# First token pair loaded by halves and projected without its norm, head norms ahead of rotations, last tile in halves

## The chip, the cores and the metric

The kernel runs on one core of a Trainium2 chip. The metric is the device time of one execution in microseconds (us), the median of several runs. The engines are TensorE (PE in the profile, with its weight loads as PEld), VectorE (DVE), ScalarE (ACT), GpSimd (POOL) and SyncE (SP), which here only issues transfers. They run side by side, each in the order of its own instructions, and wait for each other by semaphores.

## What is computed

One encoder block over 2048 tokens of width 1024 and 16 learned tokens ahead of them, in float32. Only the start and the end matter here:

```python
hn = rms_norm(h, g_mix[i])
proj = hn @ w_in[i]                      # 1024 -> 512 q, 256 k, 256 v, 512 u
q = axial_rope(rms_norm(q, g_q[i]), ...)     # norm over each head's 128
k = axial_rope(rms_norm(k, g_k[i]), ...)
attn = block_attention(q, k, v)
four = fourier_mix(u, w_fourier[i])
h = h + concat(rms_norm(attn), rms_norm(four)) @ w_out[i]
h = h + square(relu(rms_norm(h) @ w_up[i])) @ w_down[i]
return rms_norm(h, g_final)[:, N_META:]
```

`rms_norm(x, g)` is `x * rsqrt(mean(x*x) + 1e-6) * g`.

## The kernel before

**Products.** Every float32 product is made of three faster ones (`mm3`, lines 79 to 81): each operand is split into a high part (a rounded copy, `hi`) and a low part (the rest, `lo`), and high by high, high by low and low by high are added in PSUM. A split is one copy on ACT and one subtraction on DVE (`Split`, lines 69, 70; with a column of gains as a scale, 72, 73).

**Stage 1.** Tokens are taken in eight pairs `j` of two tiles `a` of 128 rows. `load_x` issues a pair's two transfers of 512 KB. `prep(j)` norms the pair (`norm_x`, for the first one `norm_first`), turns it with 16 transposes on PE (`pt`, line 290) and splits the result into `hth`, `htl`. `proj_qkv(j)` makes q, k and v from it (`pq`, `pkv`), `proj_u(j)` the Fourier input u (`pu`, copied to `UA`). `post(j, a)` is a generator that squares the heads out of PSUM, takes their norms and rotates them with DVE, transposes them on PE (`ptq`, `ptk`) and stores them. The loop at line 589 runs the generators a step at a time between the projections by `side()`, so that the work of pair `j` lies beside the projections and the preparation of pair `j+1`.

The weights `w_in` come in pieces of 256 KB (`wraw`, line 225), eight for q, k and v of rows 0 to 511 first, then eight more and eight for u; each piece is split by one ACT and one DVE instruction into `wh`, `wl`. For the first pair `proj_qkv` runs over the rows of `w_in` outermost, with all four accumulators open, so PE can begin as soon as the first pieces are split. `wake()` (line 209) gives PE six products of a constant tile ahead of everything else.

**Order.** The code is written once; a scheduler orders each engine's instructions by it and by the waits. `tc.issue_after(i)` asks that an instruction stand behind `i` on its engine. SP issues its transfers in order; at most eight are under way, and the ninth waits for the first. All raw pieces and transposed splits live in one ring of 17 buffers (`t2k`), and token tiles in one of three (`x`). PSUM has four banks `mm` for products and four `tr` for transposes in this stage.

**The end.** The down projection of the MLP is worked off in groups; the last products (name "4" of group 3) finish token tiles 4 to 7 of the second half: per tile `t` twelve products of 512 columns, `add`, and `follow`: `square` on ACT, `norm` (a small DVE instruction, then a power on POOL), and `store` of the tile before it, which scales half the row on DVE and half on ACT and issues both to SP.

## Time and profile before

| | |
|---|---|
| median of 3 runs | 2295.94 us (2295.4 to 2296.68) |
| the profiled execution's own time | 2296.3 us |
| its span, first to last instruction | 2294.5 us |
| PE busy | 2280.1 us, 99% of the span |
| DVE, ACT, POOL busy | 75%, 56%, 8% |
| granted TensorE clock over the span | 0.999 |

The profile is of one execution. Its span is 1.8 us shorter than that execution's own time, and that time is 0.36 us above the median. Busy PE is an upper bound of work, since its instructions overlap: the record of a product of 512 columns is 0.39 us long, but in the chain of waits each takes 0.23 us.

### The profile page before, as it was taken

To read this page: it belongs to the slowest core of one execution; us is meant where nothing else is said; L and a number is where in the kernel's file an instruction comes from. 1 tells how busy PE (TensorE), PEld (TensorE's weight loads), DVE (VectorE), ACT (ScalarE), POOL (GpSimd) and SP (SyncE) were. 2 spreads that over 40 slices of the span, in tenths; PEclk is the share of its full clock that TensorE was granted. 3 is DMA by queue.
4 is the path that set the end of the run, shared out by engine and by line. 5 is a ranking of instruction groups with operands and counts; after the bars stand their busy time and mean duration, and the time that the engine had idled before them with its cause. 6 is when DMAs were issued, how large, how long until landed. Compare 5 with 4: busy or idle time off the path is not lost.

```text
span 2294.5 us, 29976 instructions
## 1 busy us (share of the span) xinstructions
PE 2280.1 (99%) x10834; PEld 1882.9 (82%) x10834; DVE 1716.6 (75%) x2444; ACT 1281.7 (56%) x2303; POOL 186.9 (8%) x235
## 2 busy tenths in 40 slices
PE   9999999999999999999999999999999999999998
PEld 7888988787888888888888888888888888888887
DVE  6435579999976877976887977885884656697786
ACT  6443355566665655665765775664665555543344
POOL 2212120222000000000000100000000000200000
PEclk9999999999999999999999999999999999999999
DMA  6343252543533222333242453324454444864442
GB/s 213 100 119 103 77 169 79 164 152 119 177 117 107 93 87 79 115 113 111 93 160 79 161 172 106 97 78 167 144 171 166 151 152 156 302 197 161 129 138 83
DMA packets 178069, 307.23 MB, mean 134 GB/s; under 512 B 14960, under 2 KB 63728, under 8 KB 177536
## 3 DMA queue, kind: packets, MB, share of 16 engines
q1 hardware_dynamic: 159280, 263.16, 35.2%
q0 software_dynamic: 18640, 42.16, 6.2%
q8 instruction: 85, 1.39, 0.3%
q14 instruction: 64, 0.52, 0.1%
HBM read 225.27 MB, written 79.99 MB: 133 GB/s over the span
## 4 chain that ended last, share of the span: by engine, by line
PE 95%; DVE 2%; ACT 1%; issue 1%; DMA 1%; POOL 0%; POOLq 0%; DVEq 0%; ACTq 0%
PE pdn L79 5%; PE pdn L81 5%; PE pdn L80 5%; PE pup L79 5%; PE pup L81 5%; PE pup L80 5%; PE s L79 3%; PE ux L79 3%; PE ux L80 3%; PE ux L81 3%; PE dx L81 2%; PE dx L79 2%; PE dx L80 2%; PE s L81 2%; PE s L80 2%; PE o L79 2%
## 5 line engine op out<-in xcount | busy, mean ns | idle before, releaser
L79 PE MATMUL pdn<-wh_dn,ah 128*128 128x512 f32 x512 | 201.7, 394 | 0.5 <-ACT r L1137 0.5
L79 PE MATMUL pup<-mTh,wh_up 128*128 128x512 f32 x512 | 201.7, 394 | 0.0
L80 PE MATMUL pup<-mTl,wh_up 128*128 128x512 f32 x512 | 200.8, 392 | 0.0
L81 PE MATMUL pup<-mTh,wl_up 128*128 128x512 f32 x512 | 200.5, 392 | 0.0
L80 PE MATMUL pdn<-wl_dn,ah 128*128 128x512 f32 x512 | 200.0, 391 | 0.0
L81 PE MATMUL pdn<-wh_dn,al 128*128 128x512 f32 x512 | 198.9, 392 | 0.0
L764 ACT COPY S<-s 128x512 f32<-128x512 f32 x256 | 148.7, 583 | 53.7 <-PE s L81 40.6
L69 ACT CAST wh_up<-wr_up 128x512 fp32r<-128x512 f32 x128 | 79.4, 620 | 164.3 <-PE pup L80 76.5
L823 DVE TENSOR_TENSOR S<-S,mb 128x1024 f32<-128x1024 f32 x128 | 155.9, 1229 | 8.7 <-ACT mb L794 8.5
L70 DVE TENSOR_TENSOR pl<-S,ph 128x512 fp32r<-128x512 f32 x196 | 132.8, 698 | 11.3 <-ACT ph L69 11.0
L69 ACT CAST wh_dn<-wr_dn 128x512 fp32r<-128x512 f32 x128 | 79.0, 620 | 107.3 <-PE pdn L81 52.5
L70 DVE TENSOR_TENSOR wl_up<-wr_up,wh_up 128x512 fp32r<-128x512 f32 x128 | 87.6, 687 | 67.7 <-ACT wh_up L69 62.9
L830 DVE TENSOR_TENSOR acc<-acc,S 128x1024 f32<-128x1024 f32 x110 | 134.6, 1223 | 2.6 <-ACT S L824 2.5
L824 ACT ACTIVATE S<-S 128x1024 f32<-128x1024 f32 x114 | 120.6, 1059 | 26.2 <-DVE S L823 25.7
L70 DVE TENSOR_TENSOR wl_dn<-wr_dn,wh_dn 128x512 fp32r<-128x512 f32 x128 | 87.3, 688 | 60.4 <-ACT wh_dn L69 52.0
L69 ACT CAST ah<-a 128x1024 fp32r<-128x1024 f32 x56 | 58.5, 1048 | 121.3 <-issue 62.7
L770 DVE TENSOR_TENSOR M<-M,S 128x1024 f32<-128x1024 f32 x96 | 117.5, 1224 | 9.1 <-ACT S L764 8.7
L69 ACT CAST ph<-S 128x512 fp32r<-128x512 f32 x196 | 118.2, 620 | 8.1 <-PE o L81 5.2
L79 PEld LDWEIGHTS pdn<-wh_dn,ah 128*128 128x128 f32 x512 | 96.2, 188 | 24.0 <-ACT r L1137 3.7
L79 PE MATMUL s<-q,kt 128*128 128x512 f32 (+1 forms) x272 | 114.2, 420 | 1.4 <-DMA q<-q_d 1.4
L81 PEld LDWEIGHTS pdn<-wh_dn,al 128*128 128x128 f32 x512 | 96.2, 188 | 19.7
L79 PEld LDWEIGHTS pup<-mTh,wh_up 128*128 128x128 f32 x512 | 96.2, 188 | 19.3 <-DVE h L1163 0.2
(339 smaller groups left out, 6413.4 us busy)
## 6 DMA issues: line engine op xcount, KB each, us to landing
wr_up<-in_w_up_dram SPq DMA_DIRECT2D x128, 256.0 KB, 2.8
wr_dn<-in_w_down_dram SPq DMA_DIRECT2D x128, 256.0 KB, 2.6
a<-s_d SPq DMA_DIRECT2D x42, 512.0 KB, 3.7
R<-in_w_up_dram SPq DMA_DIRECT2D x16, 1024.0 KB, 5.4
s_d<-s SPq DMA_DIRECT2D x64, 256.0 KB, 2.1
d<-in_w_down_dram SPq DMA_DIRECT2D x26, 512.0 KB, 5.0
s_d<-c SPq DMA_DIRECT2D x48, 256.0 KB, 2.3
x<-in_x_dram SPq DMA_DIRECT2D x16, 512.0 KB, 4.9
```

Source lines behind the costliest of these rows:

```text
L69: self.high = nc.scalar.copy(hi, src)
L70: self.low = nc.vector.tensor_tensor(lo, src, f32v(hi), op=ALU.subtract)
L79: nc.tensor.matmul(out, a[0], b[0], start=first, stop=False, skip_group_check=chain)
L80: nc.tensor.matmul(out, a[0], b[1], start=False, stop=False, skip_group_check=chain)
L81: nc.tensor.matmul(out, a[1], b[0], start=False, stop=last, skip_group_check=chain)
L764: nc.scalar.copy(S[:, i % 2], ps)
L770: nc.vector.tensor_tensor(M, M, S, op=ALU.max)
L823: nc.vector.tensor_tensor(S, S, mb, op=ALU.subtract)
L824: nc.scalar.activation(p, S, AF.Exp, scale=ISQ)
L830: nc.vector.tensor_tensor(acc, acc, p, op=ALU.add)
```

## The change

Loading and projecting the first pair: its two tiles are loaded in halves of 512 columns, the first two halves ahead of the first weights and the other two behind the weights of the first 128 rows. The tiles are not normed: transposes work on the raw tiles as they land. The norm's factor `rs` is computed later (`norm_first`, now called after the weights of q, k and v were split, its squares behind the last split of the transposed tiles) and enters where the results are read: in the heads' norms (whose own mean then needs `rs` squared, `rsq_0`), in v's copy, and, spread over partitions by two transposes on PE (`spread_first`), in the copy of u, which goes from ACT to DVE for this pair. The wake products fall from six to two. ACT gets a one-element activation at the start.

`post`: squares, head norms, their products and v's copy come first, then a step of the generator ends; the table of the rotation is loaded and multiplied on POOL only then, and the rotations follow. The squares' by-product goes into `qn` rather than `t1`. For the first pair `side()` runs `prep` of the next pair ahead of the pending `post` steps.

The end: the last tile's twelve products become two runs of twelve with 256 columns, the second into a PSUM bank of its own. The first half is squared on ACT, the second on DVE. Tile 6 is stored between. The last of the stores is issued by ACT rather than SP.

```diff
-WAKE = 6
+WAKE = 2
...
+    def load_first(h):
+
+        for a in range(2):
+            if h == 0:
+                xs[0, a] = tp.tile([P, D], F32, name=f"x_0_{a}", tag="x", bufs=3)
+            c = slice(h * 512, (h + 1) * 512)
+            nc.sync.dma_start(xs[0, a][:, c], x[a * P:(a + 1) * P, c])
+
+    load_first(0)
...
         sm = tp.tile([P, 2], F32, name="sm_0", tag="sm", bufs=2)
         nc.vector.tensor_tensor(sm, ss[:, :, 0], ss[:, :, 1], op=ALU.add)
-        rs = rstd_of(tp, sm, 2, D, "x")
-        for h in range(2):
-            for a in range(2):
-                v = xs[0, a][:, h * 512:(h + 1) * 512]
-                if a == 0:
-                    early[f"x0{h}"] = ins_of(nc.scalar.activation(v, v, AF.Copy, scale=rs[:, a:a + 1]))
-                else:
-                    early[f"x1{h}"] = ins_of(nc.vector.tensor_scalar(v, v, rs[:, a:a + 1], None, op0=ALU.mult))
+        rs = rstd_of(mid, sm, 2, D, "a")
+        sq = mid.tile([P, 2], F32, name="rsq_0", tag="hsm", bufs=4)
+        nc.vector.tensor_tensor(sq, rs, rs, op=ALU.mult)
+        nc.vector.tensor_scalar(sq, sq, 1.0 / HD, None, op0=ALU.mult)
+        raw0["rs"], raw0["sq"] = rs, sq
+
+    def spread_first():
+        ps = tbank("prs_0", (P, 256))
+        for a in range(2):
+            nc.tensor.transpose(ps[:, a * P:(a + 1) * P], bc(raw0["rs"][:, a:a + 1], [P, P]), ident)
+        raw0["b"] = t2k("rsb_0", [P, 1, 256], F32)
+        nc.scalar.copy(raw0["b"][:, 0], ps)
...
-                if j < 4:
+                if j == 0:
+                    nc.vector.tensor_tensor(UA[:, g, n0:n0 + 256], ps, bc(raw0["b"], [P, 2, 256]), op=ALU.mult)
+                elif j < 4:
                     nc.scalar.copy(UA[:, g, n0:n0 + 256], ps)
...
-        rs = rstd_of(tp, ss[:rows, h0:], 6 - h0, HD, f"h{h0}", rows)
+        rs = rstd_of(tp, ss[:rows, h0:], 6 - h0, HD if j else raw0["sq"][:, a:a + 1], f"h{h0}", rows)
+        if j == 0:
+            nc.vector.tensor_scalar(rs, rs, raw0["rs"][:, a:a + 1], None, op0=ALU.mult)
...
+        if j == 0:
+            nc.scalar.activation(vr, v, AF.Copy, scale=raw0["rs"][:, a:a + 1])
+        else:
+            nc.scalar.copy(vr[:rows], v)
+        yield
+        cs = tp.tile([P, 2, P], F32, name=f"cs_{t}", tag="cs", bufs=1)
+        nc.sync.dma_start(cs[:rows], c_rope[t * P:t * P + rows, :, :])
...
     for k in range(4):
         load_w(k, 0)
         load_w(k, 512)
+        if k == 0:
+            load_first(1)
...
+            if j == 0:
+                next(nxt, None)
             for g in list(pend):
                 if next(g, "end") == "end":
                     pend.remove(g)
-            next(nxt, None)
+            if j:
+                next(nxt, None)
...
-            nc.sync.dma_start(out[(8 + t) * P:(9 + t) * P, halves[h]], w)
+            eng = nc.scalar if t == 7 and w is z else nc.sync
+            eng.dma_start(out[(8 + t) * P:(9 + t) * P, halves[h]], w)
...
+            def ends(t):
+
+                products(t, slice(0, 256))
+                rest = ybank(f"dy4_{g}_{t}")
+                products(t, slice(256, 512), rest)
+                with tc.issue_after(ends_ahead[0]):
+                    add(t)
+                h = hs[o0 + t][:, halves[half]]
+                v = h[:, 256:]
+                sq = [small.tile([P, 2], F32, name=f"ese_{i}", tag="hss", bufs=8)[:, :1] for i in range(2)]
+                nc.scalar.activation(junks[0][:, :256], h[:, :256], AF.Square, accum_out=sq[0])
+                norm_part(o0 + t, sq[0])
+                store(*done.pop())
+                nc.vector.tensor_tensor(v, v, rest[:, 256:], op=ALU.add)
+                nc.vector.scalar_tensor_tensor(junks[1][:, 256:], v, 1.0, v, op0=ALU.mult, op1=ALU.mult, accum_out=sq[1])
+                norm(o0 + t, half, sq[1])
```

SP at the start of the program, before (x are token tiles, wraw the raw pieces of `w_in`, ident the unit matrix of the transposes; a wait on a DMAHW semaphore is for an earlier transfer):

```order
L169 DMA x_0_0_90<-in_x_dram 128x1024
L169 DMA x_0_1_92<-in_x_dram 128x1024
L174 DMA cols_94<-g_cols 128x24
L176 DMA ident_96<-c_id 128x128
L225 DMA wraw0_0_141<-in_w_in_dram 128x512
L225 DMA wraw512_0_143<-in_w_in_dram 128x512
```

and now:

```order
L178 DMA x_0_0_90<-in_x_dram 128x512
L178 DMA x_0_1_92<-in_x_dram 128x512
L182 DMA cols_94<-g_cols 128x24
L184 DMA ident_96<-c_id 128x128
L236 DMA wraw0_0_139<-in_w_in_dram 128x512
L236 DMA wraw512_0_141<-in_w_in_dram 128x512
L178 DMA x_0_0_90<-in_x_dram 128x512
L178 DMA x_0_1_92<-in_x_dram 128x512
```

The first two weight pieces now stand between the halves of the token tiles, and the last half is eighth where the sixth transfer stood, with the same bytes up to its end.

PE at the middle of the first pair's transposes, now (pt are their results; before, the same 16 stand together, with waits for ACT and DVE, which scaled the tiles):

```order
L306 MATMUL pt_0_1_166<-ident_96,x_0_1_92 128x128
L306 MATMUL pt_0_2_175<-ident_96,x_0_0_90 128x128 [waits DMAHW6_49]
L306 MATMUL pt_0_3_184<-ident_96,x_0_0_90 128x128
L306 MATMUL pt_0_2_175<-ident_96,x_0_1_92 128x128 [waits DMAHW7_49]
L306 MATMUL pt_0_2_175<-ident_96,x_0_0_90 128x128
L306 MATMUL pt_0_2_175<-ident_96,x_0_1_92 128x128
L306 MATMUL pt_0_3_184<-ident_96,x_0_1_92 128x128
L306 MATMUL pt_0_3_184<-ident_96,x_0_0_90 128x128
L306 MATMUL pt_0_3_184<-ident_96,x_0_1_92 128x128
L79 MATMUL pq_0_0_334<-wh1024_0_193,hth_0_0_162 128x512 [waits Activation_49]
```

The waits are now for the transfers themselves: two transposes stand behind the third half, six behind the fourth, and all products behind these.

ACT at the norm of the third pair (jk are squares of a token tile, the x lines its scaling, qt the split of transposed q, t1 or qn the heads' squares), before:

```order
L404 ACTIVATE t1_2_822,sq_2_820<-pq_1_0_675 128x128 [waits DVE_49,PE_49]
L404 ACTIVATE t1_2_822,sq_2_820<-pq_1_0_675 128x128
L69 CAST qt_0_705<-ptq_0_700 128x512 [waits PE_49]
L244 ACTIVATE jk_2_0_0_719,ss_2_0_718<-x_2_0_664 128x512 [waits DMAHW2_49,DVE_49]
L244 ACTIVATE jk_2_0_1_721,ss_2_0_718<-x_2_0_664 128x512 [waits DVE_49]
L244 ACTIVATE jk_2_1_0_731,ss_2_1_730<-x_2_1_666 128x512 [waits DMAHW2_49,Activation_49]
L249 ACTIVATE x_2_0_664<-x_2_0_664,rs_x_727 128x1024 [waits Activation_49,Pool_49]
L244 ACTIVATE jk_2_1_1_733,ss_2_1_730<-x_2_1_666 128x512 [waits DVE_49]
L404 ACTIVATE t1_2_822,sq_2_820<-pq_1_0_675 128x128 x2
L249 ACTIVATE x_2_1_666<-x_2_1_666,rs_x_739 128x1024 [waits Activation_49,Pool_49]
```

and now:

```order
L255 ACTIVATE jk_2_0_0_725,ss_2_0_724<-x_2_0_670 128x512 [waits DMAHW5_49,DVE_49]
L69 CAST qt_0_711<-ptq_0_706 128x512 [waits PE_49]
L255 ACTIVATE jk_2_0_1_727,ss_2_0_724<-x_2_0_670 128x512 [waits DVE_49]
L255 ACTIVATE jk_2_1_0_737,ss_2_1_736<-x_2_1_672 128x512 [waits DMAHW4_49,Activation_49]
L260 ACTIVATE x_2_0_670<-x_2_0_670,rs_x_733 128x1024 [waits Activation_49,Pool_49]
L255 ACTIVATE jk_2_1_1_739,ss_2_1_736<-x_2_1_672 128x512
L260 ACTIVATE x_2_1_672<-x_2_1_672,rs_x_745 128x1024 [waits Activation_49,Pool_49]
```

One square of the third pair now stands ahead of the split of q, and the four squares of the second pair's heads stand behind the scaling of the third pair's tiles.

DVE at the end of the program, now (dx and dy4 are the last tile's sums, ers the norm's factor, epm its mean, ese the halves' sums of squares; before, the last tile has one add of 512 columns, tile 6's scaling, one epm and its own scaling):

```order
L1655 TENSOR_TENSOR hs1_18727<-hs1_18727,dx_3_3_20337 128x512 [waits PE_49]
L1616 SCALAR_TENSOR_TENSOR hs1_18727<-hs1_18727,ers_6_20841,gf0_18601 128x512 [waits Pool_49]
L1670 TENSOR_TENSOR hs1_18727<-hs1_18727,dy4_3_3_20855 128x256 [waits DVE_49,PE_49]
L1605 SCALAR_TENSOR_TENSOR epm_7_18636<-ese_0_20869,epm_7_18636 128x1 [waits Activation_49]
L1671 SCALAR_TENSOR_TENSOR ej1_18604,ese_1_20870<-hs1_18727 128x256 [waits DVE_49]
L1605 SCALAR_TENSOR_TENSOR epm_7_18636<-ese_1_20870,epm_7_18636 128x1 [waits DVE_49]
L1616 SCALAR_TENSOR_TENSOR hs1_18727<-hs1_18727,ers_7_20880,gf0_18601 128x512 [waits Pool_49]
```

The second half's square now stands behind an epm that waits for ACT's square of the first half, and on ACT (not shown) that square stands behind the scaling of tile 6.

## Rows read from the trace of the kernel before

**Rows 1.** Page, part 1: busy time, share of the span, instructions.
```profile
PE 2280.1 (99%) x10834; PEld 1882.9 (82%) x10834; DVE 1716.6 (75%) x2444; ACT 1281.7 (56%) x2303; POOL 186.9 (8%) x235
```
**Rows 2.** Waits of PE: who waited for whom: total, times, longest us.
```profile
PE pt L290 <- ACT x L249: 0.7, 1, 0.7
```
**Rows 3.** Chain of waits, first 62 us: start, length in us, what.
```profile
1.49 8.34 PE pwake L215 x12
9.82 1.75 PE pt L290 x16
11.57 0.23 PE pq L79
...
33.13 0.23 PE pkv L81
...
46.16 0.44 PE pt L290 x4
...
61.35 0.55 PE pt L290 x3
```
**Rows 4.** Timeline, first 10 us: start, length, instruction [idle before, releaser].
```profile
4.42 0.60 ACT L258 ACTIVATE jk<-x 128x512 f32<-128x512 f32 x1 [2.40 <-DMA x<-in_x_dram]
...
5.75 0.70 DVE L260 SCALAR_TENSOR_TENSOR jk<-x 128x512 f32<-128x512 f32 x1 [4.32 <-DMA x<-in_x_dram]
...
6.77 0.34 PEld L215 LDWEIGHTS pwake<-wake 128*128 128x128 f32 x1 [0.52 <-issue]
...
7.51 0.19 PEld L215 LDWEIGHTS pwake<-wake 128*128 128x128 f32 x1 [0.41 <-issue]
...
8.52 1.33 ACT L269 ACTIVATE x<-x,rs_x 128x512 f32<-128x512 f32 x2 [2.77 <-POOL rs_x L191]
```
**Rows 5.** Timeline of SP's issues at the start.
```profile
2.60 4.43 SPq L225 DMA_DIRECT2D wraw<-in_w_in_dram  x8
...
7.97 3.90 SPq L169 DMA_DIRECT2D x<-in_x_dram  x2
```
**Rows 6.** Waits of SP's queue, first 60 us: total, times, longest us.
```profile
SPq L169 <- DMA wraw<-in_w_in_dram: 0.5, 1, 0.5
```
**Rows 7.** All transfers of weight pieces `wraw`, first 35 us: from issue to landing.
```profile
DMA to landing us min/median/max: 3.4/4.4/5.5
```
**Rows 8.** Stretch 0 to 10 us: busy of each engine, granted clock, DMA share, GB/s.
```profile
0.00:10.00 10.00, 8.51 (x16) 3.76 (x17) 3.16 (x10) 4.09 (x8) 1.01 (x6) 1.00 0.83 285
```
**Rows 9.** Timeline, 28 to 47 us: reading of the first pair's products.
```profile
33.18 0.23 ACT L404 ACTIVATION_READ_ACCUMULATOR t<-pkv 128x1 f32 x1
...
33.89 1.33 POOL L191 TENSOR_TENSOR rs_h<-ms_h,mhalf 128x6 f32<-128x6 f32 x1
...
35.26 0.69 DVE L410 TENSOR_TENSOR qn<-pq,rs_h 128x512 f32<-128x512 f32 x1 [1.45 <-POOL rs_h L191]
35.87 0.41 DVE L410 TENSOR_TENSOR qn<-pkv,rs_h 128x256 f32<-128x256 f32 x1
```
**Rows 10.** Timeline of ACT, 53 to 62 us: norm of the third pair.
```profile
54.34 0.58 ACT L69 CAST qt<-ptq 128x512 fp32r<-128x512 f32 x1
...
58.94 0.26 ACT L404 ACTIVATE t<-pq 128x128 f32<-128x128 f32 x1
...
60.15 1.15 ACT L249 ACTIVATE x<-x,rs_x 128x1024 f32<-128x1024 f32 x1 [0.61 <-POOL rs_x L191]
```
**Rows 11.** Timeline of the last 9 us, all engines.
```profile
2286.30 0.55 POOL L1571 TENSOR_TENSOR ers<-epm,mhalf 128x1 f32<-128x1 f32 x1 [2.17 <-DVE epm L1569]
...
2286.82 0.39 PE L81 MATMUL dx<-bh,al 128*128 128x512 f32 x1
2287.25 0.69 DVE L1614 TENSOR_TENSOR hs<-hs,dx 128x512 f32<-128x512 f32 x1 [1.02 <-PE dx L81]
...
2288.03 0.63 ACT L1557 ACTIVATE ej<-hs 128x512 f32<-128x512 f32 x1 [1.38 <-DVE hs L1614]
...
2289.61 0.75 DVE L1576 SCALAR_TENSOR_TENSOR hs<-hs,ers,gf 128x512 f32<-128x512 f32 x1 [0.66 <-POOL ers L1571]
```

More of the change, by code (lines that the diff above doesn't have):

```diff
@@ L178, in encoder_block @@
     nc.vector.memset(ones, 1.0)
+    warm = const.tile([P, 1], F32, name="warm", tag="warm")
+    nc.scalar.activation(warm, ones, AF.Square)
     mhalf = const.tile([P, 8], F32, name="mhalf", tag="mhalf")
@@ L186, in rstd_of @@
     def rstd_of(pool, ss, n, width, tag, rows=P):
+        inv = 1.0 / width if isinstance(width, int) else width
         ms = pool.tile([P, n], F32, name="ms_" + tag, tag="ms_" + tag, bufs=2 if pool is tp else 4)
-        nc.vector.tensor_scalar(ms[:rows], ss, 1.0 / width, EPS, op0=ALU.mult, op1=ALU.add)
+        nc.vector.tensor_scalar(ms[:rows], ss, inv, EPS, op0=ALU.mult, op1=ALU.add)
         rs = pool.tile([P, n], F32, name="rs_" + tag, tag="rs_" + tag, bufs=2 if pool is tp else 4)
@@ L412, in post @@
                                     op=ALU.mult)
+        vt = t2k(f"vt_{t}", [P, 2, 2, P])
+        vr = tp.tile([P, 2, P], F32, name=f"vr_{t}", tag="vr", bufs=1)
+        v = pkv[:rows, 256:].rearrange("p (g e) -> p g e", g=2)
+        if j == 0:
+            nc.scalar.activation(vr, v, AF.Copy, scale=raw0["rs"][:, a:a + 1])
+        else:
+            nc.scalar.copy(vr[:rows], v)
+        yield
+        cs = tp.tile([P, 2, P], F32, name=f"cs_{t}", tag="cs", bufs=1)
+        nc.sync.dma_start(cs[:rows], c_rope[t * P:t * P + rows, :, :])
+        cg = tp.tile([P, 2, 2, P], F32, name=f"cg_{t}", tag="cg", bufs=1)
+        for i in range(2):
+            nc.gpsimd.tensor_tensor(cg[:rows, i], cs[:rows], gqk[:rows, i], op=ALU.mult)
+        t1 = tp.tile([P, 6, P], F32, name=f"t1_{t}", tag="t1", bufs=1)
+        for a0, a1, i in parts:
+            shape = [rows, a1 - a0, P]
             nc.vector.tensor_tensor(t1[:rows, a0:a1], qn[:rows, a0:a1], bc(cg[:rows, i, 0:1, :], shape), op=ALU.mult)
@@ L418, in post @@
             nc.vector.tensor_tensor(qn[:rows, a0:a1], t1[:rows, a0:a1], t2[:rows, :a1 - a0], op=ALU.add)
-        vt = t2k(f"vt_{t}", [P, 2, 2, P])
-        vr = tp.tile([P, 2, P], F32, name=f"vr_{t}", tag="vr", bufs=1)
-        nc.scalar.copy(vr[:rows], pkv[:rows, 256:].rearrange("p (g e) -> p g e", g=2))
         if m:
@@ L434, in post @@
                               f32v(vt.rearrange("p g l e -> p (g l) e")))
-        for _ in range(4 if j == 0 else 1):
+        for _ in range(3 if j == 0 else 0):
             yield
@@ L475, in encoder_block @@
             with ExitStack() as behind:
-                for i in ("hl" if k or c0 else ("x00", "x11")):
+                for i in "hl" if k else "h" if c0 else "":
                     behind.enter_context(tc.issue_after(early[i]))
@@ L601, in encoder_block @@
                 side()
+            spread_first()
             for a in range(2):
@@ L1566, in first, with norm_part, norm @@
         nc.vector.tensor_tensor(v, v, gfin[half], op=ALU.mult)
-    def norm(t, half):
-        nc.vector.scalar_tensor_tensor(part[t], sums[t][:, half:half + 1], 1.0 / D, part[t], op0=ALU.mult, op1=ALU.add)
+    def norm_part(t, v):
+        return ins_of(nc.vector.scalar_tensor_tensor(part[t], v, 1.0 / D, part[t], op0=ALU.mult, op1=ALU.add))
+    def norm(t, half, share=None):
+        end = norm_part(t, sums[t][:, half:half + 1] if share is None else share)
         rs = small.tile([P, 1], F32, name=f"ers_{t}", tag="rs_m", bufs=4)
@@ L1572, in norm @@
         done.append((t, half, rs))
+        return end
     def store(t, half, rs):
@@ L1588, in follow @@
                 store(*done.pop())
-        norm(t, half)
-    added = []
+        ends_ahead[:] = [norm(t, half)]
+    added, ends_ahead = [], []
     for g in range(4):
@@ L1598, in encoder_block, with products @@
             end = last and name in "374"
-            def products(t):
+            def products(t, c=slice(0, 512), apart=None):
                 if name == "1":
@@ L1604, in products @@
                     Y[t] = ybank(f"dy{name}_{g}_{t}")
-                o = (Y if name in "253" else X)[t]
+                o = (Y if name in "253" else X)[t] if apart is None else apart
                 ts = slice(t * P, (t + 1) * P)
@@ L1608, in products @@
                     a, b = ((a0, b0), (a1, b1))[k // 2]
-                    mm3(nc, o, (a[0][:, k % 2, ts], a[1][:, k % 2, ts]), (b[0][:, k % 2], b[1][:, k % 2]),
-                        name in "125" and k == 0, k == 3, True)
+                    mm3(nc, o[:, c], (a[0][:, k % 2, ts], a[1][:, k % 2, ts]), (b[0][:, k % 2, c], b[1][:, k % 2, c]),
+                        k == 0 and (name in "125" or apart is not None), k == 3, True)
             def add(t):
@@ L1637, in encoder_block @@
             else:
-                for t in range(4):
+                for t in range(3):
                     products(t)
@@ L1641, in encoder_block @@
                     follow(o0 + t, half)
+                ends(3)
                 store(*done[0])
```

27 lines of the change are left out of this document (11 added, 16 removed).

## Prediction

> **What bounds the kernel now.** I read the busy shares first: PE is busy for 2280.1 of 2294.5 us [rows 1], so only what PE waits for, at the two ends above all, can be won. The list of PE's waits holds nothing after its first instruction and before the end that is longer than 1.4 us; the one that this change touches is 0.7 us for ACT's scaling of a token tile [rows 2]. Then the chain of waits at the start [rows 3]: wake products from 1.49 to 9.82, transposes to 11.57, and from there products without a gap to 33.36. PE is the chain from 11.57 on; whatever brings the first product forward brings everything behind it forward, as long as the readers of its results keep up. Ahead of that the timeline [rows 4] shows why the transposes are not earlier: the tiles are there at 4.42 and 5.75, their norm's factor at 8.52, the scaled halves until 9.85. At the end the last product is over at 2287.21, and 2.40 us of add, square, power and handing over pass until the last scaling at 2289.61 [rows 11]; the stores and the program's end follow it.
>
> The clock matters at the start. The granted clock column says 1.00 for the first 10 us [rows 8], but the wake products' weight loads stand 0.86 us apart and take 0.34 us up to 6.77, then 0.43 apart and 0.19 [rows 4]: PE works at the lower of its two levels (1.2 GHz) until about 7.2 us, after 5.7 us of unbroken work, and at 2.4 GHz from there.
>
> **The start.** The last half of the token tiles ends at the same place in SP's stream of bytes as the sixth transfer before, the second weight piece. That one's landing is seen: SP's issue at 7.97 waited 0.5 us for it [rows 5, 6]. So I put the last half at 7.95. By the same rule, the first two halves (512 KB) land where the first whole tile did, 4.42 [rows 4], and the unit matrix and the first weight piece between the tiles' 5.75 and it, at 4.6 to 5.5. Two wake products at the lower level, four records of 0.86, end at 4.93. Eight transposes follow. At full clock a transpose takes 1.75/16 = 0.11 us [rows 3], at half clock 0.22: the eight end at 6.7. The third half, a piece of 256 KB ahead of it, lands some 0.7 earlier, by 7.25 (both of the shortest landings of rows 7, 3.4, after issues at 3.7 and 4.25, at rows 5's 0.55 each, would say 7.1 and 7.65) and frees two transposes; the fourth frees the last six at 7.95, which at full clock end at 8.6. ACT's and DVE's splits of the first pieces and tiles, 0.6 to 0.75 us each from 5.5 on, are done by then. First product 8.65 against 11.57: **2.9 us** earlier. The removed wake products and norm cost nothing on the path after that.
>
> Does the clock hold? Before, it rose under unbroken products; now there is a break of some 0.5 us from 6.7 and one of 0.5 us from 7.4, between transposes. Rows 3 show only that 1.75 us of transposes right behind products ran at the higher level; no row shows transposes raising it. The Trainium skill, "TensorE: Matmul & The Clock Gate", section "Part 4: PE-mode transpose", says that full clock does not engage for the transpose mode, which does not count as busy in the same way: a rule against this change. By that rule the clock would rise as late as in the first rival; the trace here can't decide it. I take the same 7.2 us, since PE works from 1.49 on as before but for these two breaks, and give the other case a large chance.
>
> **The reading of the first pair.** Two transposes spread `rs`: 2 x 0.11 = **0.2 us lost** on PE. Their factor is there: norm's squares stand on ACT and DVE among the splits, POOL's power is done long before PE's products end at 30.4. The squares add 2 x 0.6 us to ACT [rows 4]. Before, ACT's six squares of the first tile's heads ended at 33.41 [rows 9], so they began near 31.9 right behind the splits; now these start some 4 us earlier, held by the transfers in between, so I take the squares to begin at 31, between 30 and 32. The next thing that PE waits for is the PSUM bank of the first u, now read by DVE after much else, and needed for the last transposes of the second pair: 46.16 - 33.36 = 12.8 after the products' end [rows 3], so 30.45 + 0.2 + 12.8 = 43.5. DVE's way there: squares of six heads at 0.25 and the copy of the spread factor, 31 to 32.9; from the last square's end to the heads' product took 35.26 - 33.41 = 1.85 [rows 9], plus 0.2 for the added multiplication, so 34.95; two products (0.6, 0.35), the second tile's mean, and 1.35 of POOL's power with 0.3 of handing over bring 37.8, and seven more instructions of 0.6 and 0.33 with the read of u itself 42.4. One us of room: nothing lost, and a us per us beyond that. UA's copy moves from ACT to DVE for no cost under that cover; without the cover it would be 0.6 on the path.
>
> **The wait at 60.7.** It ended when ACT had scaled the third pair's second tile, 61.3, for the transposes at 61.35 [rows 3, 10]. From ACT's split of q at 54.34 that took 6.97; now one token square (0.6 [rows 4]) stands ahead of it and two heads' squares (0.5) behind, so 5.87, against PE's need 6.33 after the same start (60.67). The wait of 0.69 goes: **0.6 us won**; nothing is next there by my count, bounds 0 and 0.7. The transfer of that tile is behind the rotation table on SP, which POOL frees earlier than now needed.
>
> **The end.** Twenty-four products of 256 columns for twelve of 512: in the u projections four runs of 24 fill 33.36 to 46.60 with 16 transposes [rows 3], 0.12 each, so 2.87 for 2.72: **0.15 lost**. Tile 6's factor is there at 2286.85 before [rows 11], that is 0.36 ahead of the last product, now 0.5. From the last product on: ACT scales tile 6 until +0.2, squares the first half (between 0.26 for 128 columns [rows 10] and 0.63 for 512 [rows 11], so 0.4, and 0.2 to read the sum) until +0.65; DVE adds the second half (0.41 for 256 columns [rows 9]) meanwhile, takes the first mean until 0.8, squares the second half and reads the sum until 1.3, mean 1.45, POOL 0.08 + 0.55, scaling at 2.1 against 2.40: **0.3 won**. So the end gives 0.15 in all, not the whole of what the halves save, since the second square waits behind the first half's mean. The last store's issue by ACT: no row shows an ACT issue; between nothing (the last two stores are limited by their bytes, not by SP's 0.55 per issue [rows 5]) and 0.55 won, or as much lost if that queue is slower to start. I take nothing, which the SP rows are nearest to.
>
> **Sum.** 2.9 - 0.2 + 0.6 + 0.15 = 3.45 us against the profiled execution's own 2296.3: 2292.9. That execution is 0.36 above the median of the runs, which I leave in the range.
>
> **Rivals.** (1) The clock rises late. The transposes behind the last half take 1.3 instead of 0.65, first product 9.25, and the clock rises as long after it as it did after 1.49, 5.7 us, in which PE does half its work: 2.85 lost. Gain -0.05: 2296.3. For it: no row shows the clock rising over transposes or breaks. Against: PE works from 1.49 on but for two breaks of 0.5 us. (2) Slower: the same place, but the clock takes longer, as breaks go on between products waiting for splits. The point from which it decides is a rise later than 14.9 (2.83 us won without the clock, half the time lost from 9.25); at twice 5.7 us it loses 5.7 and the time is 2299.2. Against it: the pieces are there in time by my count, so PE is unbroken from 9.25. (3) The first pair's reading is late by 2 us (ACT's later start or POOL's powers), PE waits 1 to 1.5 us for the bank of u: 2294.2. For it: the room is only 1 us, and DVE has many instructions in a row. (4) The pieces land later than their bytes say, since eight smaller transfers each have an issue of their own (the eighth at 4.25) and the longest landing of a weight piece was 5.5 us [rows 7]: last half at up to 9.7, 1.7 later: 2294.6. (5) Better: landing at 7.3 and the store by ACT 0.4 earlier: 2291.8.
>
> **Chances.** The forecast 0.46 (2292.2 to 2293.6), (1) 0.24 with values between it and the forecast, (2) 0.06, (3) 0.08, (4) 0.08, (5) 0.08. Eight in ten lie between 2291.6 and 2296.5: below is half of (5), above (2) and a third of (1). A measurement of this kernel can tell about 0.2% (4.6 us) from no change: faster than 2291.35 is the end of (5) and what I overlooked, 0.07; slower than 2300.5 is the end of (2), 0.02; the same 0.91.
>
> **What would show it.** Right: the chain's first `pq` at 8.6 to 8.7 with 0.23 spacing, the transposes in two groups around 7.95, products' end near 30.4, no wait of PE for ACT's scaling near 58, and 2.1 us from the last product to the last scaling. Wrong: products 0.43 us apart beyond 9 us (1, 2), a wait of PE for DVE's `UA` near 43 (3), transposes after 8.5 (4). The forecast is wrong altogether if a later stage takes another schedule; its order of instructions is the same there.

## The result and the profile after

The changed kernel takes 2300.2 us (median of 18 runs, 2297.5 to 2304.2) against 2295.9 (18 runs, 2295.4 to 2297.7): a ratio of 1.0018, 95% interval 1.0011 to 1.0024. It is slower by 4.3 us where 3 us of gain were forecast, and its times spread over 6.7 us where the kernel before has 2.3. The profiled execution shown here is one of its fastest: 2297.79 us, 1.5 more than the profiled 2296.3 of before. So there are two things to explain: 1.5 us that even a good execution loses, and another 2.4 up to the median.

Part 1 of the page after, which answers to [rows 1]:

```profile
PE 2278.3 (99%) x10840; PEld 1882.5 (82%) x10840; DVE 1719.3 (75%) x2452; ACT 1278.6 (56%) x2301; POOL 186.5 (8%) x235
```

PE is busy for 1.8 us less than before, yet the span is 1.5 us longer: PE waits more. Its waits after (total, times, longest) show for what; the wait of [rows 2] is gone from the list:

```profile
PE pa L598 <- DVE alo L604: 2.2, 1, 2.2
PE s L79 <- DMA q<-q_d: 1.9, 2, 1.7
PE pt L306 <- DMA x<-in_x_dram: 1.8, 2, 1.6
...
PE ux L79 <- ACT p L1459: 0.5, 1, 0.5
...
PE ptq L469 <- DVE qn L450: 0.3, 1, 0.3
```

**The start.** PE's timeline, which answers to [rows 3] (start, length, instruction, idle before it and its releaser):

```profile
5.61 1.37 PE L306 MATMUL pt<-ident,x 128*128 128x128 f32 x8 [0.34 <-DMA ident<-c_id]
8.56 0.44 PE L306 MATMUL pt<-ident,x 128*128 128x128 f32 x2 [1.58 <-DMA x<-in_x_dram]
9.20 1.14 PE L306 MATMUL pt<-ident,x 128*128 128x128 f32 x6 [0.21 <-DMA x<-in_x_dram]
9.99 0.78 PE L79 MATMUL pq<-wh,hth 128*128 128x512 f32 x1
10.57 0.63 PE L80 MATMUL pq<-wl,hth 128*128 128x512 f32 x1
```

The third half of the tiles is there at 8.5 and the fourth at 9.2; between 7.0 and 8.5 PE stands still. The first products follow one another at 0.43 us. The stretches of the same execution (length; busy time and instructions of PE, of its weight loads, DVE, ACT, POOL; granted clock; DMA share; GB/s):

```profile
0.00:7.00 7.00, 5.16 (x12) 2.34 (x12) 0.54 (x2) 1.70 (x3) 0.31 (x5) 1.00 0.66 188
...
9.50:10.00 0.50, 0.50 (x7) 0.50 (x5) 0.50 (x2) 0.11 (x1) 0.00 (x0) 0.67 1.06 406
10.00:13.00 3.00, 3.00 (x9) 2.42 (x8) 2.29 (x5) 3.00 (x6) 0.00 (x0) 0.50 1.07 402
13.00:14.00 1.00, 1.00 (x5) 0.78 (x5) 1.00 (x2) 1.00 (x3) 0.00 (x0) 0.96 0.99 356
```

TensorE's granted clock, which the record has at full through the break, falls to half at 9.7, half a microsecond after the last transposes begin, and is back at 13.1: 3.4 us at 1.2 GHz instead of 2.4, with products 0.43 apart instead of 0.23. By these numbers some 1.6 us are lost (an estimate). With that the first pair's products end where they did before (0.13 us later).

**The wait for `alo`.** DVE after, then POOL after:

```profile
314.27 0.42 DVE L426 TENSOR_TENSOR qn<-pkv_m,rs_h 96x256 f32<-96x256 f32 x1 [1.62 <-POOL rs_h L202]
314.61 1.27 DVE L604 TENSOR_TENSOR alo<-pa,ahi 128x512 fp32r<-128x512 f32 x2
```

```profile
310.85 1.78 POOL L441 TENSOR_TENSOR cg<-cs,gqk 96x256 f32<-96x256 f32 x2 [4.39 <-DVE t L448]
312.58 0.92 POOL L774 DMA_DIRECT2D q<-q_d  x1
313.52 0.71 POOL L202 TENSOR_TENSOR rs_h<-ms_h,mhalf 96x2 f32<-96x2 f32 x1
```

And DVE in the kernel before, at the same place:

```profile
312.67 0.69 DVE L572 TENSOR_TENSOR alo<-pa,ahi 128x512 fp32r<-128x512 f32 x1 [0.17 <-ACT ahi L569]
313.77 0.42 DVE L410 TENSOR_TENSOR qn<-pkv_m,rs_h 96x256 f32<-96x256 f32 x1 [0.41 <-POOL rs_h L191]
314.12 0.68 DVE L572 TENSOR_TENSOR alo<-pa,ahi 128x512 fp32r<-128x512 f32 x1
```

This is the end of stage 1, 300 us behind the lines that one would look at. Because the change puts the heads' product ahead of the rotation in `post`, the scheduler also puts the product of the meta tile (`qn<-pkv_m`; the tile with the learned tokens, which comes last in this stage) one place forward on DVE, ahead of the first subtraction of the Fourier transform (`alo`). That product needs POOL's power, and POOL has a table product and the issue of a transfer (0.92 us) ahead of it. DVE waits 1.62 us with `alo` behind it, and PE, which needs `alo` for a bank, waits 2.25 us instead of 0.51. That it comes with this part of the change is seen in two runs below: d_oldstart, with the old start, has the same 2.2 us, and g_start, with nothing but the new start, 0.5.

**The end**, which answers to [rows 11]; PE's last product, then ACT, POOL, ACT:

```profile
2288.80 0.28 PE L81 MATMUL dy<-bh,al 128*128 128x256 f32 x1
2289.23 0.40 ACT L1667 ACTIVATE ej<-hs 128x256 f32<-128x256 f32 x1
...
2290.60 0.55 POOL L1610 TENSOR_TENSOR ers<-epm,mhalf 128x1 f32<-128x1 f32 x1 [2.03 <-DVE epm L1605]
...
2291.18 0.72 ACT L1617 ACTIVATE hs<-hs,ers 128x512 f32<-128x512 f32 x1 [1.46 <-POOL ers L1610]
```

From 2289.08 to 2291.18 it is 2.10 us, against 2.40 before.

**Where the time goes, along the run.** PE carries out nearly the same instructions in nearly the same order, so each can be put beside itself: its start in one trace less its start in the trace of before (positive is later). `after` is the execution above, `again` and `k1` to `k3` are four more of the same kernel (c_again, k_after1 to k_after3 below), the rest are experiments.

```
instruction at (us, before)       after  again    k1     k2     k3   a_alo0  b_wake4  d_old  e_combo  i_xfirst
29 (first pair's products)         0.13  -1.87  -0.31  -0.78   0.52  -0.05   -1.66   -0.17   -1.85    -2.48
60 (ahead of the wait at 60.7)     0.37  -1.49  -0.10  -0.56   0.75   0.17   -1.38   -0.17   -1.57    -2.19
74 (behind it)                    -0.33  -1.71  -0.80  -1.26   0.05  -0.53   -2.13   -0.87   -2.25    -2.60
293 (stage 1)                      0.19  -1.19  -0.28  -0.75   0.56  -0.01   -1.60   -0.35   -1.71    -2.07
345 (behind alo)                   1.21  -0.15   2.23   1.83   1.60  -0.07   -0.57    0.72   -2.64    -3.03
474 (behind the second q)          1.34   0.11   1.99   4.07   1.41   0.05    1.39    0.75   -2.58    -2.91
1678 (up projections)              1.08   0.50   1.60   3.68   1.39  -0.13    1.34    0.64   -2.68    -2.79
1705 (behind ACT's p)              1.71   1.37   1.94   5.46   1.92   0.89    2.09    0.96   -2.01    -2.39
2015 (down, second group)          1.71   2.77   1.94   6.67   2.68   0.89    2.10    1.34   -2.01    -2.40
own time of the execution          1.49   2.56   1.73   6.46   2.47   0.69    1.89    1.16   -2.19    -2.61
```

Steps in a column are waits or slow stretches, and between them a column is level to within some 0.3 us. That is how a loss of a few microseconds in 2300 is found. One step is the same 0.5 in all ten columns, between 74 and 293: at 263 us PE now waits 0.34 for `ptq`'s input (`ptq<-qn` in the list of waits above), since on DVE a split of the next tokens (`htl`, 0.69) now stands ahead of the rotation's last sum. Like the gain at 60.7 it comes with the heads' part of the change (d_oldstart has both), which so gives most of that gain back.

### The profile page after: what moved, and what is told of

Its sections match the earlier page's. It is cut to its first block, busy times and chain, and to the rows that moved or that the text cites. A ratio compares the mean times of both kernels' runs of the same rounds, so it can differ in the third digit from the quotient of the medians.

```text
span 2296.0 us, 29983 instructions
## 1 busy us (share of the span) xinstructions
PE 2278.3 (99%) x10840; PEld 1882.5 (82%) x10840; DVE 1719.3 (75%) x2452; ACT 1278.6 (56%) x2301; POOL 186.5 (8%) x235
## 5 line engine op out<-in xcount | busy, mean ns | idle before, releaser
L81 PEld LDWEIGHTS pup<-mTh,wl_up 128*128 128x128 f32 x512 | 96.2, 188 | 19.3
```

Of the source, the lines that this page charges most:

```text
L81: nc.tensor.matmul(out, a[1], b[0], start=False, stop=last, skip_group_check=chain)
```

## The experiments

Theory: the start gives less, since the halves land late and the clock falls behind the break; `alo` costs a steady 1 us; and what spreads the times are falls of the clock behind PE's longer breaks, in some executions and not in others. Rival: the time is lost in later stages for a reason that has to do with neither.

**c_again**: nothing changed.

> The changed kernel once more, nothing altered, for a second profiled execution and more times. Its 18 times so far have a median of 2300.2 and reach from 2297.5 to 2304.2, where the kernel before reaches from 2295.4 to 2297.7. Theory (clock): TensorE's clock falls in the break of 1.6 us in which PE waits for the third half of the first token pair, and it comes back at another time in each execution; in the first profile it was at half from 9.6 to 13.0 us. Then this execution lies above 2297.8 by half of what the low stretch is longer than 3.4 us, and PE's phases behind the first 40 us are as in the first profile. Rival (later stages): the clock is back at 13 again and what this execution has more than 2297.8 is found in waits behind 40 us. Both expect a median of 2300 +- 1.

Median 2299.6 (2298.4 to 2302.4, 11 runs), ratio 1.0016 (1.0008 to 1.0025). Its profile surprised both theories: the clock did not fall at all.

```profile
8.14 0.44 PE L306 MATMUL pt<-ident,x 128*128 128x128 f32 x2 [1.19 <-DMA x<-in_x_dram]
8.85 0.87 PE L306 MATMUL pt<-ident,x 128*128 128x128 f32 x6 [0.26 <-DMA x<-in_x_dram]
9.48 0.48 PE L79 MATMUL pq<-wh,hth 128*128 128x512 f32 x1
9.79 0.40 PE L80 MATMUL pq<-wl,hth 128*128 128x512 f32 x1
```

The first product is at 9.48, the following are 0.23 apart, 1.87 us are won at 29 us, 2.0 more than in the first execution; and still this one is 1.1 us longer. The table, column against column, says where the 3.1 us went: 0.5 at 60.7, where the wait for ACT's scaling is back, 0.8 in small steps between 345 and 1678, 0.2 behind ACT's `p` at 1698 and 1.4 at 2005 us, where PE waits for the second group of down projections. The 1.0 at `alo` and 0.6 of the wait for `p` are in both. So the start alone doesn't explain the spread.

**a_alo0**: only the order on DVE at the meta tile.

```diff
-            nc.vector.tensor_tensor(qn[:rows, a0:a1], ...)
+            with tc.issue_after(early["alo", 0, 0]) if m else nullcontext():
+                nc.vector.tensor_tensor(qn[:rows, a0:a1], ...)
```

> The changed kernel with one edit: on DVE the meta tile's heads' product is put behind the first subtraction of alo, as it stood before the change; in the changed kernel it stands ahead of it and waits for POOL's power (1.62 us in its trace), and PE's transform waits 2.25 us for alo where it waited 0.51. If that is what the wait is: PE's wait falls to 0.4 to 0.7, the time by 1.6 us to a median of 2298.6, with the spread of 6 us as it is. Rival: POOL's power itself is late (its queue has the rotation product and a DMA ahead of it), and alo's second subtraction waits as long: the wait only moves, the median stays at 2300.2.

Median 2298.8 (2294.9 to 2300.6), ratio to before 1.0009 (1.0000 to 1.0018): 0.8 less than c_again on the same chip and 1.4 less than the first set, which by the intervals could still be chance. The trace is clearer. DVE:

```profile
312.37 0.68 DVE L605 TENSOR_TENSOR alo<-pa,ahi 128x512 fp32r<-128x512 f32 x1
314.06 0.42 DVE L427 TENSOR_TENSOR qn<-pkv_m,rs_h 96x256 f32<-96x256 f32 x1 [1.02 <-POOL rs_h L202]
```

PE's wait falls from 2.2 to 1.1 in two pieces: the first `alo` is early, the second still stands behind the product that waits for POOL. Theory and rival were both partly right: the order costs what the table shows (1.0 at 345 us, none here), and POOL's queue has a part in it. To have the whole of it, all four subtractions must go ahead.

**b_wake4**: `WAKE = 4` for 2, so that PE has no long break before the first product.

> The changed kernel with four wake products for two. They end at about 8.2 us, the first eight transposes fill 8.2 to 9, the others follow at 9.2, so that PE has no break of over 0.2 us before the first product, which stays at 10. Theory (clock): the clock is up from 7.2 us on and stays; products from 10 on are 0.23 apart, 1.5 us less than in the changed kernel's first profile and 4 less than in its median: median 2296.3, spread under 2.5 us. Rival (the break does not matter, transposes or the late pieces make the clock fall or the spread comes from later stages): products 0.43 apart until 13 as before, median 2300, spread 6 us.

Median 2298.5 (2296.0 to 2300.8), ratio 1.0009 (1.0000 to 1.0018), 1.1 less than c_again. At the start the expectation held: longest break 0.3, products 0.23 apart, 1.66 won at 29 us. But the forecast median of 2296.3 left out the wait for `alo` (2.2 here too), and the clock fell elsewhere, at 459.4 us, behind a break of 2.0 that ended at 458.1. PE and then the stretches there:

```profile
458.06 0.47 PE L79 MATMUL s<-q,kt 128*128 128x512 f32 x1 [2.01 <-DMA q<-q_d]
...
459.60 0.63 PE L80 MATMUL pof<-wfl,yh 128*128 128x512 f32 x1
```

```profile
458.00:460.00 2.00, 1.94 (x9) 1.65 (x10) 1.00 (x2) 1.97 (x4) 0.00 (x0) 0.84 0.80 283
460.00:462.00 2.00, 2.00 (x6) 1.54 (x5) 1.55 (x3) 0.48 (x2) 0.00 (x0) 0.50 0.92 371
462.00:464.00 2.00, 2.00 (x10) 1.66 (x9) 0.90 (x2) 0.81 (x2) 0.00 (x0) 0.81 0.35 129
```

That wait for q stands in the kernel before as well, with 1.4 us; the trace of before has no fall there.

**d_oldstart** and **h_postfix**: the start of before, with the two other parts of the change; in h_postfix also a_alo0's edit.

```diff
-WAKE = 2
+WAKE = 6
...
-    load_first(0)
+    load_x(0)
...
```

The norm ahead of the transposes and ACT's copy of u come back with it.

> The changed kernel with the start of before: whole loads of the first pair, its norm ahead of the transposes, six wake products, u read by ACT; the heads' norms ahead of the rotations and the last tile in halves stay. Theory (clock at the start): the spread is that of before, under 2.5 us. Sum by the changed kernel's trace: 2296.0 (before) - 0.7 (wait at 60.7) + 1.6 (PE's wait for alo) + 0.5 (wait for ACT's p) - 0.3 (end) = 2297.1. Rival (later stages): the spread of 6 us stays and the median is 2299 or more.

> As d_oldstart (start of before, heads' norms ahead of the rotations, last tile in halves), and on DVE the meta tile's heads' product behind the first subtraction of alo. d_oldstart had a median of 2298.3 and waited 2.2 us for alo. Theory: the wait falls to 1.1 in two pieces, none over 0.9, and with it the chance that the clock falls behind it: median 2297.0 and spread nearer to before's 3 us. Rival: the order at alo is not what the heads' part costs; the median stays at 2298 and the spread at 3.7 us.

d_oldstart has a median of 2298.3 (2296.7 to 2300.4), 2.0 above the kernel before on its chip, ratio 1.0008 (0.9999 to 1.0017); h_postfix 2295.9 (2295.2 to 2297.8), 0.1 below it on another, ratio 1.0000 (0.9991 to 1.0009). The two differ by one place on DVE, and with the medians that place would be all that the change costs with the old start; the intervals overlap, so it is the traces that carry this: the wait is 2.2 us in the one and 1.1 in two pieces in the other, no `alo` step is left in h_postfix, and 1.1 in d_oldstart's column. The other 1.0 between the medians is not explained; it may be falls of the clock, which d_oldstart's own profile doesn't show.

**f_tail**: the kernel before with the last tile in halves alone.

> The kernel before with one part of the change alone: the last tile in halves, with its last store on ACT's queue. Prediction's term: 0.15 us won, 2296.1; by the changed kernel's trace 0.3 won, 2296.0. The spread stays that of before (2295.3 to 2298.5). Rival: the store issued by ACT opens a second hardware queue, and what the changed kernel loses at 1698 us to a late store comes from that: 0.5 us slower, and PE waits 0.5 for ACT's p at 1698.

2295.6 (2294.7 to 2297.6) against 2296.0, ratio 0.9998 (0.9989 to 1.0007): no more can be said than that it does no harm. Its profile has no wait of PE for `p` at 1698, though it has the store on ACT's queue, and g_start below has that wait (0.9) without such a store. So the store isn't what brings it, and the rival falls.

**g_start**: the kernel before with the new start alone.

> The kernel before with the new start alone: halves, two wake products, no norm ahead of the projection, factor at the reading; heads' norms after the rotations' tables as before, and the last tile whole. Theory: PE waits 0.5 for alo at 313, as before; the gain at the start is 2.1 us where the clock stays up and 0.4 where it falls for 3.4 us behind the break at 7 us, less 0.2 for the spread transposes: 2294.4 or 2296.1, and up to 1.7 more where it falls at the wait for q; median 2295.5, spread 4 us. Rival: the raw start itself delays later work (heads' norms of the first pair on DVE and POOL), so that waits of PE between 40 and 70 us take the gain back: median 2297 or more.

Median 2301.1 (2299.2 to 2304.6 but for one of the eleven executions, which took 5564 us for a reason that nothing on record shows), ratio 1.0023 (1.0014 to 1.0032), 5.2 above the kernel before: no better than the whole change. The theory missed by 5.6 us; the rival's "2297 or more" holds, and its mechanism is there, but it is a part only. The waits of its profiled execution (2304.6 us):

```profile
PE dx L79 <- DVE hs L1644: 2.6, 1, 2.6
...
PE pq L81 <- DVE htl L70: 1.2, 1, 1.2
PE ux L79 <- ACT p L1453: 0.9, 1, 0.9
```

Set beside before, PE is 0.9 us late at 29 us (its clock is at half from 7.7 to 14.6, twice as long as in the changed kernel), 2.9 late at 60: 1.8 are lost between 45 and 52 us, where `htl` of the second pair stands on DVE behind the heads of the first, as the rival had it. In the changed kernel that loss is absent. g_start lacks two things that could make the raw start bearable there: the heads' norms ahead of the rotations, and the order of `side()`, which prepares the second pair ahead of the first pair's heads. No run takes them apart. Another 4.4 go at 2005 us, 2.6 of waiting and a fall of the clock behind it.

**e_combo**: a_alo0 with all four subtractions ahead, and b_wake4.

```diff
-WAKE = 2
+WAKE = 4
-            with tc.issue_after(early["alo", 0, 0]) if m else nullcontext():
+            with tc.issue_after(early["alo", 0, 3]) if m else nullcontext():
```

> The changed kernel with four wake products for two, and with all four subtractions of alo ahead of the meta tile's heads' product on DVE (in a_alo0 only the first was, and the second waited 1.02 us for POOL's power behind that product). Theory: three breaks of PE, at the start (1.6 us), before alo (2.25) and before the second unit's q (1.4 to 2.0, in the kernel before too), each cost their length, and in some executions TensorE's clock falls behind one of them for some 3.4 us, 1.7 us more; the profile of b_wake4 showed such a fall at 458 us, behind a break of 2.0. With two of the three gone: first product at 9.9, no wait of PE at 313 over 0.3; 2296.3 - 1.6 (start) + 0.2 (spread) - 0.7 (wait at 60.7) - 0.3 (wait at 313) + 0.6 (wait for ACT's p at 1698) - 0.3 (end) = 2294.2, median up to 1 above it, and most times within 2 of each other. Rival: the two edits' gains (1.4 and 1.1 us of median) do not add, as the transfer of q is late by a fixed instant and takes back what is won ahead of it: the wait for q grows to 3 and more, the median stays at 2297 to 2298.

Median 2294.1 (2293.5 to 2296.6, ten of eleven within 1.6 us), ratio to before 0.9993 (0.9984 to 1.0002): 1.8 us below the kernel before, which the interval doesn't tell from no change, and 5 to 6 us below the changed kernel. The sum had said 2294.2. That it is met so closely is partly luck: it took 0.3 us won for the wait at 313 where the table has 0.9 between 293 and 345, and left out the 0.5 lost at 263. PE at the start, and its waits:

```profile
7.63 2.08 PE L306 MATMUL pt<-ident,x 128*128 128x128 f32 x16
9.47 0.47 PE L79 MATMUL pq<-wh,hth 128*128 128x512 f32 x1
9.78 0.39 PE L80 MATMUL pq<-wl,hth 128*128 128x512 f32 x1
```

```profile
PE s L79 <- DMA q<-q_d: 1.4, 1, 1.4
...
PE ux L79 <- ACT p L1460: 0.5, 1, 0.5
...
PE pa L599 <- DVE alo L605: 0.2, 1, 0.2
```

With two of the three breaks gone the clock stays up throughout, and the wait for q is 1.4 as before. The gain is more than a_alo0 and b_wake4 gave alone (0.8 and 1.1 below c_again); but a_alo0 moved one subtraction and this run all four, so it is not a plain sum of the two.

**i_xfirst**: e_combo with the second halves directly behind the first, `WAKE = 3`.

> e_combo with the second halves of the first pair loaded directly behind the first ones, ahead of the small tables, the unit matrix and the weights, and three wake products for four. It tests the landing term of the sum: in the changed kernel the last half landed at 9.2 us, the forecast said 7.95. In the kernel before the whole tiles had landed at 4.42 and 5.75 and the first weight piece was there well before 9. Theory (what stands ahead of the second halves in SP's stream, the small tables and the first weight piece, costs the time, not the halves' bytes): all of x by 5.8, the unit matrix by 6.6, sixteen transposes from 6.7 to 8.5 without a break, first product at 8.8 to 9.3, behind the split of the first weight piece; 0.6 to 1.1 us earlier than in e_combo: median 2293.0 to 2293.6. Rival (the order of the halves is right: the first weight piece comes as much later as x comes earlier, and its split on ACT and DVE then sets the first product): first product at 10 or later, median 2294.1 or more.

```profile
6.98 1.94 PE L307 MATMUL pt<-ident,x 128*128 128x128 f32 x16 [0.29 <-DMA ident<-c_id]
8.70 0.49 PE L79 MATMUL pq<-wh,hth 128*128 128x512 f32 x1
```

All of x is there before the unit matrix, near 7.0; sixteen transposes run at full clock without a break, and the first product is at 8.70, 0.8 earlier than in e_combo. What stood ahead of the second halves cost the time; their order in the change is a loss at the first product. The forecast median of 2293.0 to 2293.6 was not met, and against e_combo the median shows no gain: 2294.2 (2293.1 to 2297.1), ratio 0.9995 (0.9986 to 1.0004), seven times up to 2294.3 and four between 2296.4 and 2297.1. What makes those four longer no profile shows.

**k_after1** to **k_after3**: three more executions of the changed kernel.

> The changed kernel, unaltered, for a further profiled execution. Open: its median is 2.4 us above its first profile. Theory: what an execution has more than the first profile is in two things that come at random, a fall of TensorE's clock for some 3.4 us (1.7 us each) behind one of the waits for x (1.6), for alo (2.25) and for q (1.7 to 2.0), and a wait of PE for the second group of the down projections near 2005 us behind late transfers (1.1 in c_again). Sum of those against the first profile within 0.5 us. Rival: a steady difference in stages without a wait, as PE's instructions each taking longer.

> The changed kernel again; as k_after1. Theory and rival as there; a time of 2300 or more must show at least one fall of the clock besides that of the first profile, or a wait near 2005 us.

> The changed kernel again; as k_after1. Theory and rival as there.

2298.0, 2302.8 and 2298.8 us; their columns are in the table. The longest, k_after2: its waits, then its stretches behind `alo` and behind the second q.

```profile
PE s L79 <- ACT acc L860: 2.3, 1, 2.3
PE pa L598 <- DVE alo L604: 2.2, 1, 2.2
PE ux L79 <- ACT p L1459: 1.6, 1, 1.6
...
PE dx L79 <- DVE hs L1655: 0.9, 1, 0.9
```

```profile
314.00:316.00 2.00, 1.59 (x10) 1.60 (x11) 2.00 (x5) 0.72 (x3) 1.44 (x2) 0.76 1.01 185
316.00:318.00 2.00, 2.00 (x11) 2.00 (x11) 0.91 (x2) 0.88 (x2) 0.00 (x0) 0.50 1.09 311
...
460.00:462.00 2.00, 1.25 (x7) 1.14 (x8) 0.30 (x1) 1.85 (x3) 0.00 (x0) 0.95 0.53 115
462.00:464.00 2.00, 2.00 (x6) 1.54 (x5) 2.00 (x4) 0.59 (x1) 0.00 (x0) 0.50 0.99 399
```

The clock falls three times, at the start, behind `alo` and behind q. (The wait of 2.3 is put down to ACT's `acc`, which ended as PE went on, at 460.7; it is the wait for q of the other executions, whose transfer landed at 460.6. In the first execution PE starts there before that ACT instruction ends.) What a fall costs can be read from the table: between 293 and 345 us k_after1 and k_after2, which have it there, lose 2.5 and 2.6, the first execution, with the same wait and no fall, 1.0. So it is 1.5 us each. Against the first profile k_after2 loses 1.6 more at `alo` and 2.1 more at q, each with a fall, 1.2 more at 1698 and 1.2 at 2005, and has 0.9 less at the start: 5.2 by these rounded terms, for the 5.0 that it is longer. k_after3 is another case: no fall is recorded, but its products are 0.43 apart from 10.32 to 13.46, so its clock first rose there. The steady rival falls, since between its steps every column is level to within 0.3; what the theory had not listed is the wait for `p`, which varies too.

## Why the prediction was wrong

The forecast was 3.45 us won. By the table the first execution has, in its stead: 0.13 lost at the start, where 2.9 were to be won; 0.24 lost by the spread transposes; 0.70 won at 60.7; 0.52 lost at 263; 1.02 lost at `alo`; 0.13 lost up to 474, 0.26 won up to 1678, 0.63 lost for `p`; 0.22 won at the end. That is 1.49 lost. Three steps of the prediction failed: the landing of the last half, the breaks that the clock was to bear, and the order of the later stages taken as unchanged. A fourth term, the spread, was missing.

**The landing of the halves failed first.** The last half was put at 7.95 "at the same place in SP's stream of bytes as the sixth transfer before". Bytes did not set it: in the first 7 us the changed kernel moves 188 GB/s, the kernel before 238:

```profile
0.00:7.00 7.00, 5.51 (x7) 2.41 (x8) 1.79 (x5) 2.62 (x5) 0.31 (x5) 1.00 0.73 238
```

That is 0.35 MB less, 0.9 us at some 390 GB/s, the rate of later stretches; the half came at 9.2, 1.2 us late. i_xfirst, with the same halves in another order, moves 226, and has the same bytes (x, the small tables and two weight pieces) at 8.2, where the kernel before has them at 8.0. So the halving as such cost 0.2 of the 1.2 there at most. What differs is that in the change only 512 KB of x stand ahead of the small tables, the unit matrix and the first weights; which of these holds the rest up, and how, no run tells. Rival (4) had this place, up to 1.7 late, with a chance of 0.08; its reason, an issue for each of eight transfers, is not what differs from i_xfirst, which issues as many.

**The clock**, as rival (1) had feared, but not in its form. It did rise in time in four of the five executions, between 4.4 and 6.4 us; in the first, k_after1 and k_after2 it then fell again, in c_again it stayed, and in k_after3 it rose 3.2 us behind the first product. Transposes did run at full clock: in c_again PE had only the wake products, at half clock until 5.27, and eight transposes behind it when the next two took 0.10 us a load, and the record has the rise at 6.39, among the eight. The rule of the Trainium skill that the prediction weighed ("TensorE: Matmul & The Clock Gate", section "Part 4: PE-mode transpose"), that full clock does not engage for transposes, isn't what that trace shows. k_after3 would fit the rule, with all sixteen transposes at half clock and the rise only among products; whether transposes help to raise the clock, or the wake products ahead of them alone, no run separates. The step that failed is "two breaks of 0.5 us": with the late half there was one of 1.1 to 1.6 in four of the five, and the clock fell behind or in it in three of these four. In the first execution that took back what the start had won. Rival (2), the slower one, wanted a rise later than 14.9; it was at 13.5 at the latest, and the loss came from elsewhere. (The terms of rival (1) add up to 0.02 won rather than 0.05 lost, which changes nothing.)

**Spread transposes** 0.2 lost: right (0.13 to 0.36 across 33 to 36 us). **The reading of the first pair**: right, with about the room foreseen; DVE reads u at 44.73, done at 45.4, PE's transposes follow at 46.4 with no wait. g_start shows what the place is worth without the reordered heads and `side()`. **The wait at 60.7**: 0.6 foreseen, 0.70 won (0.37 to -0.33), but with luck. From ACT's split of q to the end of the scaling it is 6.36 us (54.63 to 60.99), not the 5.87 of the sum, since ACT now waits 1.12 for POOL's power ahead of the scaling where it waited 0.61 [rows 10]. That is just inside the 6.4 that PE takes. In c_again, where PE is 1.9 us earlier at 29, ACT also waits 0.99 for the tile itself, PE waits 0.48 for ACT, and only 0.22 are won. **The end**: 2.1 us from product to scaling as foreseen, 0.2 won in all for a forecast 0.15.

**"Its order of instructions is the same there"**, said of the later stages, is the step behind the losses at `alo` and at 263. It isn't: on DVE one row of the meta tile had changed places with one of the transform. The prediction had followed the heads' norms through the pairs whose waits stand in [rows 2] and stopped before the last tile, where their neighbours are other work. The wait for `alo`, 0.5 in the kernel before, was in the list of waits all along. That place costs 1.0 steadily, and 1.5 more where the clock falls behind it (two of the seven executions that have the 2.2 us wait). The 0.5 at 263 is the same kind of thing: it is in every profile with the heads' part, and in neither f_tail nor g_start.

**The spread was not in the sum at all.** The prediction costs one execution. The change made two breaks of over 1 us, at the start and before `alo`, in a kernel that had one, before q; behind each the clock may fall, at 1.5 us. The mean of the five executions is 2299.2, 1.4 above the first alone. The forecast needed a term of chance for each new break, and its range had to reach further up for them.

**Still open**: the waits for `p` at 1698 us (0.2 to 1.6) and at 2005 us (0 to 2.6). Ahead of both, DVE waits for a transfer (for a store of h at 1694: 0.54 in the first execution, 1.66 in k_after2, none in the kernel before); why it lands later is not shown. The first is in every profile with a part of stage 1 changed and in neither the kernel before nor f_tail. None of the runs took it apart. Open too is what decides whether the clock falls behind a break.

## To carry to other kernels

A reordering inside a step must be followed to the last instance of that step, where a scheduler mixes it with the next stage: compare the engines' orders to the end, and look at each in-order engine for an instruction that now waits ahead of work that PE needs. A new short break of PE costs its length and, in some executions, a stretch at half clock behind it (1.5 us here); a median then moves by more than any one profile shows, so profile a kernel whose times spread more than once. When loads are reordered, put what PE needs first in one piece ahead of the small tables (here that brought the first product forward by 0.8 us, though the median didn't show it), and don't take landing times from a count of bytes at the start of a program.

## What was not expected of the hardware

Most falls of the clock came after PE had resumed, not in the break: at 9.7 with PE back at 8.56, at 459.4 with PE back at 458.06 (instants worked out from the granted clock of their stretches). Of the ten falls in these traces eight came 0.3 to 1.3 us after; the other two, at the start of k_after2 (7.8, PE back at 7.99) and of g_start (7.7, PE back at 8.09), came at the end of the break. Whether it falls is not settled by the break alone: the same 2.2 us before `alo` was followed by a fall in two of seven profiles, the breaks of 2.0 and 2.3 before q in both, those of 1.2 to 1.8 there in none; at the start one of 1.19 was not (c_again) and one of 1.15 was (k_after1). Nor does the record of the granted clock show the state that a program starts in: k_after3's says 1.00 for the first 13 us, with weight loads of 0.33 us and products 0.43 apart up to 13.46.
